# A row softmax on one core: chunks of 7 rows per partition instead of 8, with one chunk of 2 rows at the end

## The chip, the cores and the metric

One core of a Trainium2 chip runs the kernel. The metric is the device time of one execution in microseconds (us); within a group of runs, the slowest execution of one kernel is above its fastest (162.9 to 163.22 us, 0.2%, for the kernel before). The span of a profile is somewhat shorter than the device time of the same execution (161.3 us against 163.08 us for the kernel before).

## The reference

A softmax over the last axis of a float32 array of 16 x 1024 x 512, that is 16384 rows of 512 numbers:

```python
def reference(x):
    x_max = np.max(x, axis=-1, keepdims=True)
    exp_x = np.exp(x - x_max)
    return (exp_x / np.sum(exp_x, axis=-1, keepdims=True)).astype(np.float32)
```

33.55 MB are read and 33.55 MB are written. Each number is used three times on the chip: by a maximum, an exponential with a row sum, and a multiplication.

## The kernel before

The 16384 rows are 128 rows for each of 128 partitions. A chunk is R rows per partition, here always 8; it is loaded, worked on in place and stored from the same tile. There are 12 tiles of 8 rows (12 x 16 KB per partition).

```python
CHUNKS = [8] * 16
SLOTS = {8: 12}
# ... (cut: views of x and out by chunk, "(p r) d -> p r d" with r=R)

def load(k):
    R = CHUNKS[k]
    tiles[k] = data.tile([P, R, d], F32, name=f"x{R}", tag=f"x{R}", bufs=SLOTS[R])
    nc.sync.dma_start(out=tiles[k], in_=src[k])

def rowmax(k):     # VectorE: minus the maximum of each row
    # ... (cut)
    nc.vector.reduce_max(out=shift[k], in_=tiles[k], axis=AX, negate=True)

def exps(k):       # ScalarE: R times exp(x - max), with the row's sum
    # ... (cut) nc.scalar.activation(..., func=EXP, bias=shift, accum_out=sums)

def scale(k):      # VectorE: 1/sum, then R multiplications
    # ... (cut) nc.vector.reciprocal(...); nc.vector.tensor_scalar_mul(...)

def store(k):
    nc.scalar.dma_start(out=dst[k], in_=tiles[k])

for k in range(K):
    load(k); rowmax(k); exps(k)
    if k >= 1:
        scale(k - 1); store(k - 1)
scale(K - 1); store(K - 1)
```

A load and a store of a chunk have one packet per partition: R rows of 2 KB that lie next to each other, so 16 KB for 8 rows. In the trace of the kernel before each queue has 2048 packets of 16384 bytes and 256 of 4 bytes for its 16 transfers: 128 packets and 16 completion words for a transfer, so 8 packets (8 of the 128 partitions) and one word of 4 bytes for each of the 16 DMA engines. The issue records in the trace name eight completion semaphores (counters that a transfer raises when it is done, and on which others wait), which the transfers use in turn. No transfer is issued before its semaphore shows that its earlier user has landed, 0.3 to 0.6 us after that one's last completion word (24 such pairs in the kernel before), and about half are issued within 0.1 us of it (12). So a store can wait for a load that has nothing to do with it.

Of the kernel before, what the change touches and what calls it, by code (L numbers as in the profile page):

```python
# [1 line left out]

# [4 lines left out]

F32 = mybir.dt.float32
EXP = mybir.ActivationFunctionType.Exp
AX = mybir.AxisListType.X  # L10


CHUNKS = [8] * 16

SLOTS = {8: 12}


@with_exitstack
def kernel(
    ctx: ExitStack,  # L20
    tc: tile.TileContext,
    x: bass.AP,
    out: bass.AP,
):
    nc = tc.nc
    P = nc.NUM_PARTITIONS

    x_flat = x.flatten_outer_dims()
    out_flat = out.flatten_outer_dims()
    n, d = x_flat.shape  # L30
    assert n == P * sum(CHUNKS)


    src, dst, at = [], [], 0
    for R in CHUNKS:
        for flat, views in ((x_flat, src), (out_flat, dst)):
            part = flat[at : at + P * R, :]
            views.append(part.rearrange("(p r) d -> p r d", r=R))
        at += P * R

    data = ctx.enter_context(tc.tile_pool(name="data", bufs=1))
    stats = ctx.enter_context(tc.tile_pool(name="stats", bufs=4))

    K = len(CHUNKS)
    tiles = [None] * K
    shift = [None] * K
    sums = [None] * K
# [6 lines that stand above are left out]
    def rowmax(k):  # L54
        R = CHUNKS[k]
        shift[k] = stats.tile([P, R], F32, name=f"shift{R}", tag=f"shift{R}")
        nc.vector.reduce_max(out=shift[k], in_=tiles[k], axis=AX, negate=True)  # L57

    def exps(k):
        R = CHUNKS[k]  # L60
        sums[k] = stats.tile([P, R], F32, name=f"sums{R}", tag=f"sums{R}")
        for r in range(R):
            nc.scalar.activation(  # L63
                out=tiles[k][:, r, :],
                in_=tiles[k][:, r, :],
                func=EXP,
                bias=shift[k][:, r : r + 1],
                scale=1.0,
                accum_out=sums[k][:, r : r + 1],
            )  # L70

    def scale(k):
        R = CHUNKS[k]
        recip = stats.tile([P, R], F32, name=f"recip{R}", tag=f"recip{R}")
        nc.vector.reciprocal(out=recip, in_=sums[k])  # L75
        for r in range(R):
            nc.vector.tensor_scalar_mul(  # L77
                out=tiles[k][:, r, :],
                in0=tiles[k][:, r, :],
                scalar1=recip[:, r : r + 1],  # L80
            )

    def store(k):
        nc.scalar.dma_start(out=dst[k], in_=tiles[k])  # L84

    with tc.manual_schedule():
        for k in range(K):
            load(k)
            rowmax(k)
            exps(k)  # L90
            if k >= 1:
                scale(k - 1)
                store(k - 1)
        scale(K - 1)
        store(K - 1)


# [1 line left out]
_INS = ['x']  # L99
_OUTS = [((16, 1024, 512), 'float32')]  # L100


# [23 lines left out]
```

## Time and profile before

| | kernel before |
|---|---|
| time, median of 4 runs (lowest to highest) | 163.06 us (162.9 to 163.22) |
| span of the profiled run | 161.3 us |
| bytes moved, mean rate over the span | 67.14 MB, 416 GB/s |
| VectorE / ScalarE busy | 77% / 58% |
| last store issued / last completion | 149.5 us / 160.2 us |

The first fence holds lines of the page of the kernel before: busy engine time, the 40 slices of the span (a digit is the busy share in tenths, GB/s is what the DMA engines moved), and the two DMA queues, q1 the loads and q10 the stores, with the time of their packets as a share of 16 engines' span.

```profile
DVE 123.8 (77%) x160; ACT 93.2 (58%) x257; POOL 0.2 (0%) x4
...
DVE  0088799999999999985970079999999999957000
...
DMA  6999999999999999999999999999999999999993
GB/s 163 431 427 427 431 435 378 418 445 431 423 439 431 421 435 431 431 439 418 439 435 427 431 427 435 435 425 435 431 427 439 431 427 427 431 435 431 431 435 171
...
q1 hardware_dynamic: 2304, 33.56, 49.5%
q10 hardware_dynamic: 2304, 33.56, 48.6%
```

The DMA row is 9 from the second slice to the last but one, nearly always at 420 to 440 GB/s: the transfers are the limit. The two queues' shares add to 98.1% of the span, 158.2 us of work for each engine. VectorE is full in two stretches only and rests in between.

The chain of waits of the kernel before, as shares of the span by engine, then the longest waits of ScalarE and VectorE (in total, times, longest):

```profile
DMA 52%; DVE 31%; ACT 6%; SPq 2%; issue 1%; ACTq 1%; DVEq 0%
```

```profile
ACT x L63 <- DMA x<-in_x_dram: 18.6, 2, 12.1
DVE recip L75 <- ACT x L63: 15.3, 4, 10.1
DVE shift L57 <- DMA x<-in_x_dram: 9.7, 3, 8.6
```

The chain goes back from the last instruction that the profile counts, and this is a multiplication of VectorE, not the last store. So the 31% for VectorE are not 31% that a faster VectorE would save. The 18.6 us of ScalarE waiting for loads are not a lack of data either: they are stores at the head of ScalarE's queue that wait for a semaphore which a load still holds. By the trace's records load 8 lands at 68.9 us and store 5, which uses its semaphore next, is issued at 69.5; load 10 lands at 86.9 and store 6 is issued at 87.4. Both stores' data had long been ready: VectorE ended the multiplications of chunk 5 at 61.0 us and those of chunk 6 at 68.8.

Two more views show how much VectorE has to spare at the end. The issues of the stores (first and last start), then busy time of the engines, DMA share and GB/s in four stretches:

```profile
L84 ACTq DMA_DIRECT2D out_dram<-x x16: 338/338/374, 22.4 to 149.5; - x16
```

```profile
144.00:148.00 4.00, 2.01 (x6) 1.92 (x6) 0.00 (x0) 1.00 1.01 430
148.00:152.00 4.00, 1.46 (x4) 0.00 (x0) 0.00 (x0) 1.00 1.01 430
152.00:156.00 4.00, 0.00 (x0) 0.00 (x0) 0.00 (x0) 1.00 1.02 438
156.00:160.00 4.00, 0.00 (x0) 0.00 (x0) 0.00 (x0) 1.00 0.72 307
```

The last store is issued at 149.5 us, and the engines stay full for another nine: they have a backlog of earlier stores. By the completion records the store before it ends between 153.9 us on the first engine and 155.3 us on the last one.

### The profile page before, as it was taken

The page shows a single profiled execution, that of the slowest core. Times are in us where ns is not written, and L with a number is a line of the kernel's source. Part 1 is how long each engine was busy: PE and PEld are TensorE (multiplying, and loading weights), DVE is VectorE, ACT ScalarE, POOL GpSimd, SP SyncE. Part 2 cuts the span into 40 slices and gives each one's busy share as a digit, 9 for nine tenths or more (in the row PEclk, how much of TensorE's full clock was granted, in tenths as well). Part 3 has the DMA queues.
Part 4 walks back from the last instruction along what each step waited for, and adds up shares of the span by engine and source line. Part 5 has one row for each costly group of instructions (what it writes and reads, how often), then busy time and mean ns, then how long its engine had stood idle before and what let it go on. Part 6 is the DMA issues. An engine that isn't in the chain of part 4 may idle for free.

```text
span 161.3 us, 527 instructions
## 1 busy us (share of the span) xinstructions
DVE 123.8 (77%) x160; ACT 93.2 (58%) x257; POOL 0.2 (0%) x4
## 2 busy tenths in 40 slices
DVE  0088799999999999985970079999999999957000
ACT  0037994959596867067002996859595959591000
POOL 0000000000000000000000000000000000000000
DMA  6999999999999999999999999999999999999993
GB/s 163 431 427 427 431 435 378 418 445 431 423 439 431 421 435 431 431 439 418 439 435 427 431 427 435 435 425 435 431 427 439 431 427 427 431 435 431 431 435 171
DMA packets 4612, 67.14 MB, mean 416 GB/s; under 512 B 513, under 2 KB 513, under 8 KB 513
## 3 DMA queue, kind: packets, MB, share of 16 engines
q1 hardware_dynamic: 2304, 33.56, 49.5%
q10 hardware_dynamic: 2304, 33.56, 48.6%
q14 instruction: 4, 0.02, 0.0%
HBM read 33.55 MB, written 33.55 MB: 416 GB/s over the span
## 4 chain that ended last, share of the span: by engine, by line
DMA 52%; DVE 31%; ACT 6%; SPq 2%; issue 1%; ACTq 1%; DVEq 0%
DMA x<-in_x_dram 52%; DVE shift L57 16%; DVE x L77 14%; ACT x L63 6%; SPq L52 2%; DVE recip L75 1%; ACTq L84 0%; DVEq L121 0%; ACTq L63 0%
## 5 line engine op out<-in xcount | busy, mean ns | idle before, releaser
L63 ACT ACTIVATE x<-x,shift 128x512 f32<-128x512 f32 x128 | 90.5, 709 | 44.1 <-DVE shift L57 21.4
L57 DVE TENSOR_REDUCE shift<-x 128x8 f32<-128x4096 f32 x16 | 70.6, 4415 | 9.7 <-DMA x<-in_x_dram 9.7
L77 DVE TENSOR_SCALAR x<-x,recip 128x512 f32<-128x512 f32 x128 | 52.1, 482 | 0.6
L63 ACT ACTIVATION_READ_ACCUMULATOR x<-x,shift 128x1 f32 x128 | 24.0, 187 | 0.0
L75 DVE RECIPROCAL recip<-sums 128x8 f32<-128x8 f32 x16 | 3.1, 196 | 15.3 <-ACT x L63 15.3
L63 ACT ACT_TABLE_LOAD x1 | 1.3, 1283 | 8.7 <-DMA x<-in_x_dram 8.7
L110 POOL MEMSET const-bfloat16-1.0<- 128x1 bf16 x1 | 0.1, 102 | 0.0
L110 POOL MEMSET const-uint8-127<- 128x1 uint8 x1 | 0.1, 102 | 0.0
L110 POOL MEMSET const-float32-0.0<- 128x1 f32 x1 | 0.1, 99 | 0.2 <-issue 0.2
L110 POOL MEMSET const-float32-1.0<- 128x1 f32 x1 | 0.1, 99 | 0.0
## 6 DMA issues: line engine op xcount, KB each, us to landing
x<-in_x_dram SPq DMA_DIRECT2D x16, 2048.0 KB, 42.6
out_dram<-x ACTq DMA_DIRECT2D x16, 2048.0 KB, 18.0
```

The lines of the kernel that those rows point to most:

```text
L52: nc.sync.dma_start(out=tiles[k], in_=src[k])
L57: nc.vector.reduce_max(out=shift[k], in_=tiles[k], axis=AX, negate=True)
L63: nc.scalar.activation(out=tiles[k][:, r, :], in_=tiles[k][:, r, :], func=EXP, bias=shift[k][:, r : r + 1], scale=1.0, accum_out=sums[k][: ...
L75: nc.vector.reciprocal(out=recip, in_=sums[k])
L77: nc.vector.tensor_scalar_mul(out=tiles[k][:, r, :], in0=tiles[k][:, r, :], scalar1=recip[:, r : r + 1],)
L110: nc = _bacc.Bacc("TRN2", target_bir_lowering=False, num_devices=1)
```

## The change

The idea is to use chunks of 7 rows, so that the pipeline starts earlier and has finer steps, and to end with 2 rows, so that little compute is left after the last load. 18 x 7 + 2 = 128 rows per partition.

```diff
-CHUNKS = [8] * 16
+CHUNKS = [7] * 18 + [2]
 
-SLOTS = {8: 12}
+SLOTS = {7: 13, 2: 1}
```

## The prediction

> **What bounds the kernel now.** The transfers. In the page's slices the 16 DMA engines are full from the second slice to the next-to-last, at 420 to 440 GB/s, mean 416 over the span; VectorE is busy 77%, ScalarE 58%. The trace's DMA records show engines full from 1.7 us to 160.2 us of the 161.3 us span: loads take 79.8 us per engine, stores 78.2. That is 67.1 MB at about 430 GB/s. [...] The chain of waits names DVE for the last 68 us, but stores queue behind it: the last one is issued at 149.5 us, while the store before it lands at 155.3 us. So VectorE has some 2 to 4 us to spare at the end, not zero.
>
> **What the change moves.**
> - Bytes and exps: unchanged.
> - Packets: one per partition and chunk, 16384 B, 611 ns; a completion write of 4 B takes 9 ns. 611 - 9 = 602 ns is bytes, so about 9 ns per packet is fixed. Per engine and direction there are 152 packets instead of 128 and 19 completion writes instead of 16: 27 x 9 ns = 0.24 us, or +0.5 us for both directions, all on the critical path.
> - VectorE: three more reduces and reciprocals. About 0.15 us fixed per reduce and 0.12 to 0.2 us per reciprocal give +0.9 us of 123.8. Off the critical path unless the store backlog runs dry.
> - Start: the first chunk lands about 0.6 us sooner, the first store is issued near 20 us instead of 22.4. Worth nothing while loads fill the engines anyway.
> - End: a last chunk of 2 rows helps only if its compute is exposed; it is not.
>
> **The risk.** DMAs share eight completion semaphores in rotation, so a store can wait for a load that used its semaphore before. Before, stores 5, 6, 7 waited for loads 8, 10, 11 (ACT idle 6.5 and 12.1 us; VectorE's 10.1 us idle before the reciprocal). In the changed program's order, store 7 waits for load 12, store 9 for load 14, store 10 for load 15: further ahead, and stores 12, 13, 15 wait for loads 16, 17, 18. Held stores cost nothing while loads fill the engines, but VectorE's multiplies slip with them. After the loads end (132 us before), stores alone drain a 7-row chunk in about 4.3 us (4.86 x 7/8), while VectorE makes one every 6.8 us (7.73 before). The backlog must last. I expect the spare at the end to shrink to about zero, costing 0 to 2 us.
>
> **Prediction.** 163.08 + 0.5 (packets) + about 0.4 (expected end gap) = 164.0 us, 8 in 10 between 163.0 and 166.0. Faster by over 2%: 2%; within 2%: 91%; slower by over 2%: 7%.
>
> **What would show it.** Packets of 14336 B at 536 ns; per-engine sum of transfer time up 0.5 us; DMA slices still full in the middle; more VectorE idle time before the reciprocal, one ScalarE wait still near 12 us; last store issued within 4 us of 152 us.
>
> **What would make it wrong.** 14 KB packets[...] could run slower or faster than bytes say: 1% of packet time is 1.6 us. The semaphore rotation could starve the end by more than 2 us.

## The result

| | before | changed |
|---|---|---|
| time, median of 4 runs each | 163.06 us | 163.83 us (163.73 to 163.97) |
| ratio, 95% interval | | 1.0048, 1.003 to 1.0065: within 2% |
| span of the profiled run | 161.3 us | 162.0 us |
| last store issued / last completion | 149.5 / 160.2 us | 154.4 / 160.7 us |

The same lines of the changed kernel's page, with its chain:

```profile
DVE 124.7 (77%) x166; ACT 93.2 (58%) x257; POOL 0.2 (0%) x4
...
DVE  0099799999999999592049229999789999998810
...
DMA  5999999999999999999999999999999999999994
GB/s 159 435 428 425 439 354 414 427 435 414 446 435 420 435 414 442 435 425 435 425 432 435 425 432 435 425 434 425 428 443 421 428 426 444 421 435 418 418 407 200
...
q1 hardware_dynamic: 2736, 33.56, 49.6%
q10 hardware_dynamic: 2736, 33.56, 48.5%
...
DMA 55%; DVE 29%; ACT 8%; issue 2%; ACTq 0%; DVEq 0%; SPq 0%
```

The engines are full as before. The two queues' shares again add to 98.1%, of a span that is 0.7 us longer: the engines worked longer, they did not rest longer. (The shares count recorded durations, long ones too: the first packets of the changed kernel are recorded with up to 2.45 us, where the median of its 14 KB packets is 0.535.)

Its waits, its store issues and the same four stretches:

```profile
ACT x L63 <- DMA x<-in_x_dram: 27.6, 4, 11.1
DVE recip L75 <- ACT x L63: 20.1, 6, 9.2
...
DVE shift L57 <- DMA x<-in_x_dram: 9.0, 3, 8.4
```

```profile
L84 ACTq DMA_DIRECT2D out_dram<-x x19: 338/338/375, 20.5 to 154.4; - x19
```

```profile
144.00:148.00 4.00, 3.96 (x9) 2.76 (x8) 0.00 (x0) 1.00 1.02 437
148.00:152.00 4.00, 2.92 (x7) 3.70 (x12) 0.00 (x0) 1.00 1.01 434
152.00:156.00 4.00, 2.37 (x7) 0.00 (x0) 0.00 (x0) 1.00 0.92 391
156.00:160.00 4.00, 0.00 (x0) 0.00 (x0) 0.00 (x0) 1.00 0.95 396
```

ScalarE waits 9 us more for loads (27.6 against 18.6 us) and VectorE 4.8 us more for ScalarE. The longest ones are again stores held by a load's semaphore: store 7 is issued at 90.5 us, just after load 12, five chunks ahead of it, lands at 90.1. The last store is issued 4.9 us later than before. In the stretch from 152 to 156 us the engines are no longer full: 391 GB/s instead of 438. This is the gap that the prediction feared. By the completion records it did not reach the end: the first engines end the last two stores of 7 rows at 153.6 and 158.6 us, 5.02 us apart, where the stores before follow each other every 4.26 us: they rested for about 0.76 us. The last of the 16 engines ends them at 155.2 and 159.5 us, 4.26 us apart, so it did not rest at all. The slowest engine sets the time: SyncE's wait for the last store ends at 161.07 us, 0.35 us after that engine's last completion (160.72), and the program ends at 161.99.

To see what did add to the time, I cut each span in three from the trace's transfer records. "Packets" is the number of packets per engine times their median duration, with 9 ns for each completion word. "Rest" is the last completion less the packets: the start, stalls, and gaps of the slowest engine. "Close" is from the last completion to the end of the span.

| profiled run | span | packets | rest | close |
|---|---|---|---|---|
| before | 161.31 | 156.70 | 3.47 | 1.13 |
| changed | 161.99 | 156.97 | 3.75 | 1.27 |
| difference | 0.69 | 0.27 | 0.28 | 0.14 |

The profiled run of the changed kernel was also the slowest of its four (163.97 us), so its rest may be a little larger than usual.

One warning about the column "packets": recorded durations overlap. A packet of 16 KB is recorded with 611 ns, but the next one of the same engine starts 607 ns after it; for 14 KB it is 535 and 532, for 8 KB (e1 below) 309 and 306. So the column is about 1.1 us too large in both kernels, and rest as much too small. The differences between kernels with these chunk sizes are hardly touched (by less than 0.06 us). Where the number of packets differs much (e1, e8, e12), the pace is the better measure: in the stretch where only stores remain, the completions of one transfer after the other come every 4.862 us for 8 rows, 4.260 for 7 rows, 4.900 for 8 rows in two packets per partition (e1) and 9.681 for 16 rows (e12). Two transfers of 8 rows take 9.725 us, so eight packets and their completion word cost 44 ns beside their bytes (9.725 - 9.681); eight packets alone cost 38 ns (4.900 - 4.862), which is about 5 ns for one. The change has six transfers more: 6 x 44 ns = 0.26 us, as the column says.

Close has a plain cause. At the end SyncE waits for the eight semaphores in the same order in both traces, about 62 ns for a step whose wait is already met (161.07, 161.13 and 161.20 us in the changed kernel). In the kernel before, the last store used the last semaphore of this order; in the changed kernel it used an earlier one, and two more waits stand behind it. The rest is there from the first chunk on: the slowest engine's first completion is 3.37 us later than its 8 packets alone would need in the kernel before, 3.72 us in the changed one. Two of the first packets take 2.4 us there, against 1.9 us at most before.

### The profile page after: what moved, and what is told of

The parts are those of the page before. It is cut to its first block, busy times and chain, and to the rows that moved or that the text cites. A ratio compares the mean times of both kernels' runs of the same rounds, so it can differ in the third digit from the quotient of the medians.

```text
span 162.0 us, 547 instructions
## 1 busy us (share of the span) xinstructions
DVE 124.7 (77%) x166; ACT 93.2 (58%) x257; POOL 0.2 (0%) x4
## 4 chain that ended last, share of the span: by engine, by line
DMA 55%; DVE 29%; ACT 8%; issue 2%; ACTq 0%; DVEq 0%; SPq 0%
DMA x<-in_x_dram 55%; DVE x L77 14%; DVE shift L57 14%; ACT x L63 8%; DVE recip L75 1%; ACTq L84 0%; DVEq L121 0%; SPq L52 0%; ACTq L63 0%
## 5 line engine op out<-in xcount | busy, mean ns | idle before, releaser
L63 ACT ACTIVATE x<-x,shift 128x512 f32<-128x512 f32 x128 | 90.5, 708 | 50.1 <-DMA x<-in_x_dram 27.6
L57 DVE TENSOR_REDUCE shift<-x 128x7 f32<-128x3584 f32 (+1 forms) x19 | 71.0, 3739 | 9.0 <-DMA x<-in_x_dram 9.0
L75 DVE RECIPROCAL recip<-sums 128x7 f32<-128x7 f32 (+1 forms) x19 | 3.6, 192 | 20.1 <-ACT x L63 20.1
```

Of the source, the lines that this page charges most:

```text
L63: nc.scalar.activation(out=tiles[k][:, r, :], in_=tiles[k][:, r, :], func=EXP, bias=shift[k][:, r : r + 1], scale=1.0, accum_out=sums[k][: ...
L75: nc.vector.reciprocal(out=recip, in_=sums[k])
```

## The experiments

Theory A: the change pays for more packets; a packet costs a fixed time whatever its size. Rival B: it pays at the end, where the backlog of stores runs short. Theory S came up after the first four runs, for the part that A does not explain. All runs gave right results, and each had 5 rounds. The kernel before measured 163.03 us in the first group of four runs, 163.29 us in the second and 163.14 us in the third (e9 to e12, on another chip), so ratios are safer than differences between groups. Where CHUNKS changes, SLOTS changes with it (cut below), so the number of tiles is not held fixed: 12 before, 14 in the changed kernel, 12 to 14 in the others of this kind.

### e1: the same chunks, packets cut in two

```diff
+        pad = data.tile([P, 2, R // 2 * d + 8], F32, ...)   # a gap of 32 bytes between the halves
+        tiles[k] = pad[:, :, : R // 2 * d]
+        nc.sync.dma_start(out=tiles[k], in_=src[k].rearrange("p (h r) d -> p h (r d)", h=2))
# ... (cut: the store in the same way, and the row views of the compute)
```

> The kernel before, chunks of 8 rows unchanged, but every tile padded between its two halves, so that each transfer is cut into packets of 8 KB instead of 16 KB: 128 more packets per engine and direction, nothing else. Theory A (a fixed cost of about 9 ns per packet is what the change paid): 2 x 128 x 9 ns = +2.3 us, so about 165.4 us, packets of 8 KB at 310 ns. Theory B (the change paid at the end, where the store backlog ran short): packets cost nothing apart from their bytes, so within 0.3 us of 163.06.

164.51 us, ratio 1.0089 (1.0076 to 1.0103). The DMA lines of its page:

```profile
DMA packets 8707, 67.14 MB, mean 413 GB/s; under 512 B 512, under 2 KB 512, under 8 KB 512
...
q1 hardware_dynamic: 4352, 33.56, 49.6%
q10 hardware_dynamic: 4352, 33.56, 48.7%
```

Twice the packets for the same bytes cost 1.48 us, with the same chunks and the same semaphores. B fails for this kernel, A holds in kind. Its size was too large: by the records' durations a packet costs 2 x 309 - 611 = 7 ns, and by the pace, which the overlap does not touch, about 5 ns (4.7), not 9. 256 packets are then 1.2 us of the 1.3 us by which the profiled span grew. One side effect: SyncE takes longer to issue a load (0.61 us against 0.37 for the first), and the first packet starts at 2.12 us instead of 1.74.

### e2: the chunk of 2 rows first

```diff
-CHUNKS = [7] * 18 + [2]
+CHUNKS = [2] + [7] * 18
```

> The changed kernel with the chunk of 2 rows at the start instead of the end: the same number of packets of the same sizes, another end (a last chunk of 7 rows, whose exps and multiplies are exposed longer) and another order of the shared semaphores. Theory A (packets): within 0.3 us of the changed kernel, 163.8. Theory B (end of the store backlog): the end is longer by at least part of the 5 more rows of exps and multiplies (about 6 us of work), so 164.8 to 167 us.

163.42 us, ratio 1.0022 (1.0008 to 1.0035). The same packets as the change, and half of its loss. The cut of its span shows why: packets 156.97 and close 1.26, both as in the changed kernel, but rest 3.42, as before. So packets and close together cost 0.39 us, both by the profile and by the clock, and the other part of the change's loss is the rest. The expectation of B, over 164.8 us, is clearly missed. That of A (within 0.3 us of the changed kernel's 163.8) is missed by 0.1 us too: packets alone are not the whole loss.

### e3 and e4: more work for VectorE at the end of each kernel

```diff
# ... (cut: with again=True, rowmax writes the same maxima a second time)
             rowmax(k)
+            if k == K - 2:          # e3, from the kernel before; K - 3 in e4, from the changed one
+                rowmax(k, again=True)
```

> The kernel before with the row maximum of chunk 14 (the last but one) computed twice, which puts 4.4 us more of VectorE work before the last stores. If the kernel before has 2 to 4 us to spare at its end, as the prediction says: +0 to +1.5 us. If it has none: +4.4 us.

> The changed kernel with the row maximum of chunk 16 (9 rows before the end) computed twice, 3.8 us more of VectorE work. If the change used up the spare time at the end (store 17 was issued 0.9 us before the engines could start it, and the slowest engine was not yet idle): +2.3 to +3.8 us against the changed kernel, so 166.1 to 167.6. If spare time is left as before: +0 to +1.5 us.

e3: 162.97 us, ratio 0.9998 (0.9985 to 1.001). The 4.4 us cost nothing. e4: 167.04 us, ratio 1.0244 (1.023 to 1.0258), against 1.0048 for the changed kernel: 3.2 us more (0.0196 of 163.06) for 3.88 us of work. The end of e3, then of e4:

```profile
148.00:152.00 4.00, 1.72 (x5) 2.21 (x8) 0.00 (x0) 1.00 0.96 410
152.00:156.00 4.00, 1.74 (x5) 0.00 (x0) 0.00 (x0) 1.00 0.95 401
156.00:160.00 4.00, 0.00 (x0) 0.00 (x0) 0.00 (x0) 1.00 0.80 340
```

```profile
148.00:152.00 4.00, 3.96 (x10) 3.16 (x9) 0.00 (x0) 1.00 0.54 229
152.00:156.00 4.00, 2.93 (x7) 3.30 (x10) 0.00 (x0) 1.00 0.93 394
156.00:160.00 4.00, 1.98 (x6) 0.00 (x0) 0.00 (x0) 1.00 0.70 294
160.00:164.00 4.00, 0.00 (x0) 0.00 (x0) 0.00 (x0) 1.00 0.87 360
```

In e3 the store backlog hides the delay (401 GB/s at the least until 156 us). In e4 the engines fall to 229 GB/s. This is the change's real effect, and the time hardly shows it: before, VectorE had over 4 us to spare at the end; after, it had about 0.7 us (3.88 less 3.2, give or take 0.4 by the intervals).

### e5 and e6: two chunks of 8 first, or last

```diff
-CHUNKS = [8] * 16
+CHUNKS = [8] * 2 + [7] * 16     # e5;   e6: [7] * 16 + [8] * 2
```

> Chunks [8]*2 + [7]*16: a third chunk size mix with 16 packets per engine and direction more than before (the change had 24), no chunk of 2, and a start with packets of 16 KB. In the profiles so far the change's 0.69 us of span split into about 0.25 us of packet time and completion writes, 0.30 us of a later slowest engine that is there from the first chunk on, and 0.13 us at the program's end (after the last completion). Theory S (the 0.30 us comes with the size of the very first packets): 163.03 + 0.16 (packets and completion writes) + 0 to 0.13 = 163.2 to 163.35. Theory B (it comes from the small last chunk or the thin store backlog at the end): the same here, so this run needs the next one beside it.

> The same chunks in the other order, [7]*16 + [8]*2, so the same packets, but a start with packets of 14 KB and an end with 8 rows. Theory S (first packets): 0.3 us over the run with the eights first, 163.5 to 163.65, with the slowest engine's first completion write as late against its packets' time as in the changed kernel. Theory B (2-row chunk at the end): equal to the run with the eights first within 0.15 us.

e5: 164.24 us, ratio 1.0064 (1.0052 to 1.0076); e6: 163.85 us, ratio 1.0035 (1.0022 to 1.0048). The order is the opposite of the one that S expects. For e5 the stretches of the end tell why:

```profile
148.00:152.00 4.00, 2.34 (x6) 4.00 (x13) 0.00 (x0) 1.00 0.94 401
152.00:156.00 4.00, 3.06 (x8) 0.47 (x2) 0.00 (x0) 1.00 0.84 355
156.00:160.00 4.00, 0.00 (x0) 0.00 (x0) 0.00 (x0) 1.00 0.95 401
```

Here all engines starve: the last store is issued at 155.6 us, and all 16 engines end it within 0.15 us, while in the kernel before they are 1.4 us apart. In this run the end without a backlog lined the engines up. So B, wrong for the change itself, is right one chunk order further. e5's span splits into packets 156.84, rest 4.12, close 1.45 (four waits stand behind its last store, 0.25 us at 62 ns each). The first packets do agree with S (none over 1.68 us in e5; up to 2.27 us in e6, rest 3.71), but the two times can't test it, because e5 has an end of its own.

### e7: only the small chunk at the end

```diff
-CHUNKS = [8] * 16
+CHUNKS = [8] * 15 + [6, 2]
```

> Chunks [8]*15 + [6, 2]: the start, packet sizes and order of before, and only the change's 2-row chunk at the end. Theory A (packets) with S (first packets): 8 more packets per engine and direction at 7 to 9 ns, +0.1 to 0.15 us, and up to 0.13 us at the program's end: 163.1 to 163.3. Theory B (the 2-row chunk at the end costs the change 0.4 us): 163.4 or more.

163.38 us, ratio 1.0006 (0.9992 to 1.002). By the ratio it is as A expects; the median lies between the two expectations, because the whole group ran slower. The 2-row chunk at the end neither helps nor costs.

### e8: loads in pairs

```diff
# ... (cut: the views of x and out, now of 16 rows)
-        tiles[k] = data.tile([P, R, d], ...)
-        nc.sync.dma_start(out=tiles[k], in_=src[k])
+        if k % 2 == 0:
+            both = data.tile([P, 2 * R, d], ..., bufs=SLOTS[R] // 2)
+            nc.sync.dma_start(out=both, in_=src[k])      # src[k] is now a view of 16 rows
+            tiles[k] = both[:, :R, :]
+            tiles[k + 1] = both[:, R:, :]
```

> The kernel before with its loads joined in pairs, 16 rows per partition and load (packets of 32 KB), while maxima, exps, multiplies and stores keep chunks of 8 rows: 64 packets and 8 completion writes fewer per engine. Theory A: 64 x 7 ns + 8 x 9 ns = 0.5 us less than before, 162.5, if the later first landing (about 4.9 us) is hidden. If packets cost nothing fixed: 163.0. If the later start shortens the store backlog at the end: over 163.5.

162.71 us, ratio 0.9969 (0.9957 to 0.9981), as A expects. Its waits and store issues are instructive:

```profile
ACT x L73 <- DVE shift L67: 27.2, 13, 3.1
...
DVE recip L85 <- ACT x L73: 4.0, 2, 2.5
```

```profile
L94 ACTq DMA_DIRECT2D out_dram<-x x16: 338/338/376, 26.7 to 140.9; - x16
```

With half as many loads the turn of the eight semaphores falls otherwise, and no store has to wait for a load that is still on its way. In the list of waits no line has a ScalarE exponential wait for a load (18.6 us before), VectorE waits 4.0 us for ScalarE instead of 15.3, and the last store is issued at 140.9 us, 8.6 us earlier than before. The gain is 0.5 us (0.3 to 0.7 by the interval), and eight transfers fewer at 44 ns explain 0.35 us of it. Work that is ready 8.6 us sooner, behind full DMA engines, was worth little or nothing here.

### e9, e10, e11: is it the size of the first packets?

```diff
-CHUNKS = [7] * 18 + [2]              # the changed kernel
+CHUNKS = [8, 6] + [7] * 16 + [2]     # e9
-CHUNKS = [8] * 16                    # the kernel before
+CHUNKS = [7, 9] + [8] * 14           # e10
+CHUNKS = [9, 7] + [8] * 14           # e11
```

> The changed kernel with its first two chunks of 7 and 7 rows made 8 and 6: 19 chunks as in the change, the same number of packets, the same end, but a start with packets of 16 KB. The runs so far: the three kernels that start with 14 KB packets have some first packets of 2.2 to 2.45 us and their slowest engine 0.3 to 0.4 us later from the first chunk on; the four that start with 16 KB have none over 1.91 us. Theory S (the size of the first packets): 0.3 us less than the changed kernel, a ratio to the kernel before of 1.002 to 1.003, no first packet over 1.95 us. If the start is not the cause: a ratio of 1.0045 to 1.005, as the changed kernel.

> The kernel before with its first two chunks of 8 and 8 rows made 7 and 9: 16 chunks and as many packets as before, but a start with packets of 14 KB. Theory S: 0.2 to 0.4 us over the kernel before, and over the next run; first packets of over 2.1 us. If the start is not the cause: within 0.15 us of before.

> The control of the run before: first chunks of 9 and 7 rows, the same packets in another order, a start with packets of 18 KB. Theory S, if it is 14 KB that is slow and not any size other than 16 KB: within 0.15 us of the kernel before. If any departure from 16 KB is slow: as the run before.

e9: 163.56 us, ratio 1.0027 (1.0012 to 1.0043). e10: 163.05 us, ratio 0.9996 (0.9981 to 1.001). e11: 163.27 us, ratio 1.0006 (0.9991 to 1.0021). e9 came out as S wants it in time, though its profiled run, the slowest of its six at 163.97 us, had a first packet of 2.18 us and a rest of 3.70. e10 speaks against S: a start with 14 KB cost nothing, and no first packet went over 1.81 us. In e11 the rest was 3.64 us, with no loss in the ratio. So the rest moves by 0.3 us between kernels, and within one too: e3, e10 and the kernel before start and end much alike and have 3.23, 3.36 and 3.47. S in its simple form falls; what sets the rest stays open.

### e12: loads and stores in pairs

```diff
# ... (cut: the loads in pairs, as in e8)
+        if k >= K - 2:
+            half = slice(0, R) if k % 2 == 0 else slice(R, 2 * R)
+            nc.scalar.dma_start(out=dst[k][:, half, :], in_=tiles[k])
+        elif k % 2 == 1:
+            nc.scalar.dma_start(out=dst[k], in_=pairs[k])    # 16 rows
```

> The paired loads of the run e8 and paired stores too (packets of 32 KB; only the last two stores stay single): 56 packets and 7 completion writes fewer per engine than e8, at 9 ns each (two packets of 16 KB at 611 ns against one of 32 KB at 1213 ns). Theory A: 0.55 us less than e8, so 1.1 us under the kernel before (ratio 0.993 to 0.994), the fastest of all. If the later stores leave the engines without work: more than that.

162.33 us, ratio 0.9952 (0.9937 to 0.9966): the fastest kernel here, 0.8 us under the kernel before, which is still within the 2% that count as the same. Its queues:

```profile
q1 hardware_dynamic: 1152, 33.55, 49.3%
q10 hardware_dynamic: 1296, 33.56, 48.5%
```

This is less than the expected 1.1 us, which took 9 ns for a packet. By the pace, 15 transfers fewer than in the kernel before are worth 15 x 44 ns = 0.66 us, and the ratio gives 0.78 us (0.55 to 1.03). So the fixed cost per packet accounts for most of the gain, and the larger saving that the recorded durations suggest (1.21 us) is their overlap.

## Why the prediction was right

It said 164.0 us (163.0 to 166.0), within 2%; measured was 163.83. Point by point:

- **The transfers are the limit: right.** The engines are as full after as before, and e3 (ratio 0.9998), e7 (1.0006) and e8 (0.9969, most of it fewer transfers) show that here earlier or later compute did not count as long as the backlog held.
- **Packets, +0.5 us: right in kind, too large.** The term was mis-sized because the 9 ns of a 4-byte completion word were taken for the fixed part of a large packet. The pace of packets of 16 and 8 KB gives about 5 ns. A 14 KB packet took 535 ns (536 predicted), and packets with completion words came to +0.27 us.
- **VectorE, +0.9 us and off the critical path: right.** 123.8 to 124.7 us busy. A maximum took 4.415 us for 8 rows, 3.880 for 7 and 1.212 for 2: 0.534 us a row and about 0.145 fixed (0.15 predicted). A reciprocal took 0.154 us for 2 rows to 0.196 for 8.
- **The start: right in that it is worth nothing.** The first store was issued at 20.5 us (near 20 predicted), but the first chunk landed 0.25 us sooner (8.01 against 8.26 us) and not 0.6.
- **The semaphores: right.** VectorE's wait before the reciprocal grew from 15.3 to 20.1 us, the longest ScalarE wait for a load was 11.1 us, and the last store was issued at 154.4 us, within 4 us of 152.
- **The spare time at the end shrinks to about zero: right. That it costs about 0.4 us: wrong for the profiled run.** e3 and e4 measured the spare time: over 4 us before (the prediction said 2 to 4), about 0.7 us after. Fast engines rested for about 0.76 us, but the slowest did not, and it sets the end: the gap cost nothing there. e2 and e9, with the same packets, lost 0.4 us, as much as packets and close cost.
- **What it missed.** Neither close (+0.14 us) nor the later start of the slowest engine (in the rest, +0.28 us in the profiled run) was in the prediction. These two happened to fill the place of the too large packets and of the end gap. So the bound, the direction and the vanished reserve were foreseen, but that the total came within 0.2 us was luck: it was better than its terms.

What stays open is the +0.28 us of rest: it is in the profiles of the changed kernel, e6 and e9, it is not in that of e2, and the size of the first chunk alone (e10) does not bring it. Nor was it tested by itself that the semaphore waits, and not the finer chunks, put the last store of the changed kernel 4.9 us later; this is read from the waits. It was not tested either what sets the distance between the 16 engines: they are 0.8 us apart after the first load of the kernel before already (7.43 to 8.26 us), and 1.4 us at its end.

The fixed cost of a packet is small as a share (about 5 ns by the pace, under 1% of the 611 ns of a 16 KB packet), but with the engines full it is a part of what the change paid, and most of what e8 and e12 gained.

## What to carry to other kernels

Here the DMA engines were full from end to end, and the finer pipeline won nothing and paid for its packets (0.27 us). In such a kernel count the packets, and try larger ones (here 0.5% for 32 KB). An unchanged time can hide a lost reserve; adding known work to the end of both kernels measures it (here over 4 us fell to 0.7 us). And where transfers share completion semaphores in turn, as here, look at which store waits for which load after a change of the number of chunks: ScalarE waited 18.6 us for loads in the kernel before, 27.6 us in the changed one, and no exponential waited for a load in e8.
